# Two-layer hybrid decoder trunk on Trainium2: gating activations, a sliding tile's row maximum and the order of filler work and gated tiles changed

## Chip, cores and metric
The kernel runs on one core of one Trainium2 chip. The metric is the device time of one execution in microseconds, here the median of three runs. The engines are TensorE (PE, with PEld for its weight loads), VectorE (DVE), ScalarE (ACT), GpSimd (POOL) and SyncE (SP), whose queue issues nearly all DMA.

## What is computed
Two layers over 1024 positions of width 1024. Each layer projects once, runs three causal token mixers on parts of the projection, gates each and sums the three; then comes an output projection, a norm and a second gated addition (cut here).

```python
u = rms_norm(x, norm_pre[l]) @ w_in[l]
(a_q, a_k, a_v, a_z, b_q, b_kv, b_kr, b_z, c_q, c_k, c_v, c_z, g) = split(u)
oa = diff_attention(...)              # 4 heads, two softmaxes each
ob = mla_attention(...)               # 8 heads, low-rank keys and values
oc = sliding_window_attention(...)    # 8 heads, 128 keys back, a sink in the softmax
gates = sigmoid(g).reshape(B, S, 3, D)
y = (gates[:, :, 0] * ((oa * silu(a_z)) @ w_br_a[l])
     + gates[:, :, 1] * ((ob * silu(b_z)) @ w_br_b[l])
     + gates[:, :, 2] * ((oc * silu(c_z)) @ w_br_c[l]))
x = x + rms_norm(y @ w_out[l], norm_post[l])
```

## The kernel before
Everything is kept transposed, channels on partitions, positions along the free axis in two halves (`hf`) of 512. A product in fp32 is made of three fast matmuls: each operand is split (`split`, L88) into a high part H (a cast on ACT) and a low part L = x - H (DVE, L93), and HH + HL + LH are summed in PSUM. PSUM has eight banks: two with the tag mm, three sc, two tr, one av.

A layer runs through these stages:
- **Dense stage.** Four `z_unit`s (L434) make z of mixer a: 128 channels each, 48 matmuls of 128x512, an evacuation (zs) by ACT, a store to DRAM. Then `seven` (L458) prepares sums and differences T of the hidden state and runs eight `pair`s (L484). A pair makes 256 channels with seven products instead of eight, 84 matmuls: in the bank X twice with weight block 1 (`wr` w1), in Y with S2, S3 and A22, in Z with S1 and S4, all made from w1 and a second raw block w2. u2, u3 and p1 (tiles `po`) collect X, Y and Z. Here the pairs make gates 0 and 1.
- **sw** (L627): 16 sliding tiles. Each makes scores of four heads in two sc banks (L689), adds the bias (L691), takes the maximum (L692, with the sink at L697), exponentiates on ACT (L703), transposes and multiplies by the values.
- **da** (L813), then **mla** (L922), which begins with `mla_entry` (L1008). Each mixer ends with `put_rows` (L605): reciprocals of its row sums are transposed on PE and stored.
- **merge** (L1096): for each of the three mixers 16 `gated` tiles (8 j and hf; four channel blocks by two halves), then eight column blocks of 128, two halves each, 12 matmuls per half: 192 matmuls a mixer. `gated` loads o, z and the reciprocals rb, forms o * rb * silu(z) and splits it.
- **tail**: output projection and the second gate.

Beside the mixers run **fillers**: generators of dense units (here z of b and c, gate 2: 16 units of 48 matmuls). `fill` (L335) advances them by six matmuls at places in the mixers; FILL gives how many steps at which place and RATE which share of them goes to these units. What is left is drained at the start of the merge.

A scheduler puts each engine's instructions into a fixed order from the order in the program; what stands under `high_priority` comes earlier. At run time every engine, and SP's queue, takes its instructions in that order, so one that waits holds up all behind it.

Of the kernel before, what the change touches and what calls it, by code (L numbers as in the profile page):

```python
# [60 lines left out]
class Builder:  # L61
# [372 lines left out]
    def z_unit(self, l, b, j):  # L434
        W = self.load_w(self.win(l, OFF[b + "z"] + j * P))

        def evac(hf, ps):
            st = self.zp.tile([P, 512], F32, tag="zs", bufs=2, name=self.uid("zs"))
            self.copy("a", st, ps)
            self.nc.sync.dma_start(  # L440
                self.z_d[l, b][j * P:(j + 1) * P, hf * 512:(hf + 1) * 512], st)

        yield from self.unit(W, KT, self.hT, evac)

    def g_unit(self, l, bi, j):
        W = self.load_w(self.win(l, OFF["g"] + bi * D + j * P))
# [11 lines left out]
    def seven(self, l):  # L458
        nc = self.nc
        with ExitStack() as ctx:  # L460
            pl = self.pool("seven", ctx)
            T = [[tuple(pl.tile([P, 512], F32R, name=self.uid("T")) for _ in range(2))
                  for _ in range(4)] for _ in range(4)]
            for k in range(4):
                r = {}
                for hf in range(2):
                    for c in range(2):
                        H, L = self.hT[hf][4 * c + k]
                        r[c, hf] = pl.tile([P, 512], F32, tag="po", bufs=5, name=self.uid("po"))
# [10 lines left out]
            for bi in range(2):  # L480
                for j in range(0, KT, 2):
                    self.drain(self.pair(l, pl, T, OFF["g"] + bi * D + j * P, self.g_d, bi * D + j * P))

    def pair(self, l, pl, T, c, dst, r0):  # L484
# [5 lines left out]
        w1, w2 = self.load_raw(self.win(l, c)), self.load_raw(self.win(l, c + P), pl, tag="s")  # L490
# [36 lines left out]
        def put(a, hf, src):  # L527
            nc.sync.dma_start(dst[r0 + a * P:r0 + (a + 1) * P, hf * 512:(hf + 1) * 512], src)
# [24 lines left out]
        with self.tc.high_priority():  # L553
# [73 lines left out]
    def sw(self, l):  # L627
        nc = self.nc
        with ExitStack() as ctx:
# [13 lines left out]
            R = pl.tile([P, 8, 8], F32, name=self.uid("R"))  # L643
# [30 lines left out]
            self.put_rows(pl, l, "c", R.rearrange("p h i -> p (h i)"))  # L674
            self.fill(FILL[5], True)

    def sw_tile(self, l, pl, g, i, bias, sink, qs, kA, kB, Vp):
# [6 lines left out]
        for c in range(2):  # L684
# [6 lines left out]
            nc.vector.tensor_tensor(ps[:, :, k0:], ps[:, :, k0:], bias[:, h0:h0 + 2, k0:], ALU.add)  # L691
            nc.vector.tensor_reduce(mx[:, 2 * c:2 * c + 2], ps[:, :, k0:], AX.X, ALU.max)  # L692
# [4 lines left out]
        nc.vector.tensor_tensor(mx, mx, sk, ALU.max)  # L697
# [618 lines left out]
```

## Time and profile before

| | before |
|---|---|
| median of 3 runs | 2736.88 us (2733.1 to 2738.93) |
| profiled execution | 2740.26 us |
| its span | 2738.5 us |
| mean granted TensorE clock | 0.984 |
| PE busy | 2619.7 us, 96% |
| DVE busy | 1703.1 us, 62% |
| ACT busy | 1265.1 us, 46% |
| POOL busy | 393.2 us, 14% |

A busy time is the union of an engine's instructions. PE's share of 96% is a mean over stages: in some it is busy for whole stretches, in others it waits, and the granted clock tells where the chip let it run below full speed. The rows name a tile by the program's name with its buffer number left out, so `sc<-sc,swb` is the sliding tile's bias add.

### The profile page before, as it was taken

The page shows a single profiled execution, that of the slowest core. Times are in us where ns is not written, and L with a number is a line of the kernel's source. Part 1 is how long each engine was busy: PE and PEld are TensorE (multiplying, and loading weights), DVE is VectorE, ACT ScalarE, POOL GpSimd, SP SyncE. Part 2 cuts the span into 40 slices and gives each one's busy share as a digit, 9 for nine tenths or more (in the row PEclk, how much of TensorE's full clock was granted, in tenths as well). Part 3 has the DMA queues.
Part 4 walks back from the last instruction along what each step waited for, and adds up shares of the span by engine and source line. Part 5 has one row for each costly group of instructions (what it writes and reads, how often), then busy time and mean ns, then how long its engine had stood idle before and what let it go on. Part 6 is the DMA issues. An engine that isn't in the chain of part 4 may idle for free.

```text
span 2738.5 us, 35853 instructions
## 1 busy us (share of the span) xinstructions
PE 2619.7 (96%) x12832; PEld 2132.5 (78%) x12832; DVE 1703.1 (62%) x3232; ACT 1265.1 (46%) x2759; POOL 393.2 (14%) x359
## 2 busy tenths in 40 slices
PE   8999979999999988999999999899999999889999
PEld 6888758887877866788878887688887877668887
DVE  8653665776587655655566537567756876456653
ACT  5322543555477643334443226445545765333332
POOL 2000000000010034315410000000000111351441
PEclk9999979999999999999999999999999999999999
DMA  6333222211011376443333331222110114764442
GB/s 207 99 112 85 64 51 63 66 49 59 24 31 27 91 236 212 145 141 119 125 120 100 112 85 53 80 57 58 53 54 21 28 42 154 238 191 130 139 121 93
DMA packets 296818, 269.21 MB, mean 98 GB/s; under 512 B 24272, under 2 KB 237456, under 8 KB 296512
## 3 DMA queue, kind: packets, MB, share of 16 engines
q1 hardware_dynamic: 295568, 262.19, 31.8%
q0 software_dynamic: 1072, 4.73, 0.6%
q8 instruction: 101, 1.65, 0.3%
q14 instruction: 77, 0.63, 0.1%
HBM read 194.93 MB, written 61.44 MB: 94 GB/s over the span
## 4 chain that ended last, share of the span: by engine, by line
PE 76%; DVE 9%; DMA 5%; ACT 4%; issue 3%; POOL 2%; SPq 0%; DVEq 0%; POOLq 0%; ACTq 0%
PE mm L305 44%; PE sc L104 8%; PE mm L519 8%; PE av L774 5%; PE tr L790 3%; PE sc L519 3%; DVE wL L93 2%; PE sc L305 2%; ACT wH L78 1%; DVE o L1159 1%; PE tr L711 1%; POOL o L1158 1%; DVE po L473 1%; DMA wr<-w_in 1%; DMA sig<-g_d 1%
## 5 line engine op out<-in xcount | busy, mean ns | idle before, releaser
L305 PE MATMUL mm<-big,wH 128*128 128x512 f32 x3456 | 1111.9, 397 | 23.3 <-ACT zs L78 14.2
L305 PEld LDWEIGHTS mm<-big,wH 128*128 128x128 f32 x3456 | 642.4, 189 | 152.8 <-ACT zs L78 19.7
L305 PE MATMUL mm<-big,wL 128*128 128x512 f32 x1728 | 683.4, 396 | 3.3 <-DVE wL L93 3.2
L93 DVE TENSOR_TENSOR wL<-wr,wH 128x1024 fp32r<-128x1024 f32 (+3 forms) x252 | 268.7, 1073 | 246.2 <-ACT wH L78 238.5
L305 PEld LDWEIGHTS mm<-big,wL 128*128 128x128 f32 x1728 | 326.6, 189 | 66.6 <-DVE wL L93 4.5
L78 ACT CAST wH<-wr 128x1024 fp32r<-128x1024 f32 (+3 forms) x252 | 211.9, 851 | 289.2 <-PE mm L305 231.7
L761 ACT ACTIVATE e<-sc,st 128x512 f32<-128x512 f32 (+3 forms) x384 | 221.7, 582 | 96.1 <-DVE st L758 62.7
L755 DVE TENSOR_REDUCE st<-sc 128x1 f32<-128x512 f32 (+3 forms) x384 | 208.6, 551 | 5.8 <-PE sc L104 1.7
L78 ACT CAST wtH<-tr 128x512 fp32r<-128x512 f32 x204 | 115.5, 589 | 94.1 <-PE tr L790 72.4
L790 PE MATMUL tr<-cm,e 128*128 128x128 f32 x864 | 148.9, 275 | 1.1 <-ACT e L761 1.0
L93 DVE TENSOR_TENSOR wtL<-tr,wtH 128x512 fp32r<-128x512 f32 x204 | 137.7, 681 | 15.0 <-ACT wtH L78 13.7
L305 PE MATMUL mm<-oH,wH 128*128 128x512 f32 x256 | 103.6, 405 | 20.6 <-DVE y L1128 14.8
L790 PEld LDWEIGHTS tr<-cm,e 128*128 128x128 f32 x864 | 107.2, 142 | 19.6 <-ACT e L761 6.9
L519 PE MATMUL mm<-T,aH 128*128 128x512 f32 x384 | 119.0, 390 | 1.2 <-ACT T L78 1.1
L104 PE MATMUL sc<-kA,q 128*128 128x256 f32 (+3 forms) x320 | 106.2, 343 | 0.4
L305 PE MATMUL mm<-oL,wH 128*128 128x512 f32 x256 | 102.4, 400 | 0.0
L305 PE MATMUL mm<-oH,wL 128*128 128x512 f32 x256 | 102.0, 399 | 0.0
L104 PE MATMUL sc<-kB,q 128*128 128x256 f32 (+3 forms) x320 | 100.4, 323 | 0.0
L305 PE MATMUL mm<-og,wH 128*128 128x512 f32 x256 | 83.6, 409 | 13.6 <-DVE sig L1130 8.9
L1159 DVE TENSOR_TENSOR o<-o,sg 128x512 f32<-128x512 f32 x48 | 52.6, 1099 | 67.7 <-POOL o L1158 62.5
L1154 POOL TENSOR_TENSOR sg<-sg,z 128x512 f32<-128x512 f32 x48 | 70.2, 1466 | 169.3 <-ACT sg L1153 169.0
L78 ACT CAST aH<-S 128x512 fp32r<-128x512 f32 x64 | 39.5, 622 | 107.5 <-PE mm L519 63.7
(306 smaller groups left out, 4930.2 us busy)
## 6 DMA issues: line engine op xcount, KB each, us to landing
wr<-w_in SPq DMA_DIRECT2D x108, 512.0 KB, 3.9
sig<-g_d SPq DMA_DIRECT2D x48, 512.0 KB, 3.7
wr<-w_out SPq DMA_DIRECT2D x32, 512.0 KB, 4.1
wr<-w_ple_gate SPq DMA_DIRECT2D x32, 512.0 KB, 4.0
g_d<-zs SPq DMA_DIRECT2D x48, 256.0 KB, 2.2
g_d<-po SPq DMA_DIRECT2D x48, 256.0 KB, 2.2
kB<-kA SPq DMA_DIRECT2D x80, 128.0 KB, 2.7
x<-x SPq DMA_DIRECT2D x16, 512.0 KB, 6.1
```

What stands on the lines that cost most here:

```text
L78: nc.scalar.copy(out, in_)
L93: (nc.vector if le == "v" else nc.gpsimd).tensor_tensor(L, src, h, ALU.subtract)
L104: self.nc.tensor.matmul(ps, w, x, start=i == 0, stop=i == n - 1)
L305: self.nc.tensor.matmul(ps, w, x, start=i == 0, stop=i == n - 1)
L473: nc.vector.tensor_tensor(out, x, y, ALU.subtract)
L519: nc.tensor.matmul(ps, w, x, start=start and not i, stop=i == 11, skip_group_check=True)
L755: nc.vector.tensor_reduce(st[:, c:c + 1], ps[:, :w], AX.X, ALU.max, negate=len(ch) == 1)
L761: nc.scalar.activation(e[:, k0:k0 + w], pss[c][:, :w], AF.Exp, bias=st[:, 0:1], accum_out=sums[:, c:c + 1])
L774: self.nc.tensor.matmul(av[:, 0:256], w, x, start=self.first and not i, stop=last and i == len(terms) - 1)
L790: self.nc.tensor.transpose(tr[:, (2 * a + q) * P:(2 * a + q + 1) * P], ws[q][:, kt * P:(kt + 1) * P], self.ident)
L1154: nc.gpsimd.tensor_tensor(sg, sg, z, ALU.mult)
L1159: nc.vector.tensor_tensor(o, o, sg, ALU.mult)
```

## The change
- **Activations.** `z_unit` (now of mixer a alone) stores silu(z): sigmoid on ACT, product on DVE. The pairs now make z of b and c, with a sigmoid on ACT and a product on GpSimd, and gate 0, with its sigmoid. The fillers are gates 1 and 2, their weights' low halves on GpSimd (`le="g"`). The merge takes the sigmoid only for those two.
- **The pair.** The product Z x S1 is written ahead of Y x S3; the second raw weight block has one buffer instead of two, the split parts three instead of four.
- **Sliding tiles.** Bias sum and maximum are one instruction per head, which starts from the sink; the step with the sink alone is gone. RATE for this part is 1.0 instead of 0.5.
- **Row sums.** The transposes of c and a are put off (`rows_due`) to behind the next stage's first group, with filler in between.
- **Merge.** `gated` has two parts: the loads, with GpSimd's o * rb, and the rest. The first part runs two tiles ahead, tiles of the next mixer are made during the present one, weight blocks are loaded two column blocks ahead, and the products rotate over seven banks.

The diff, cut to what the text below speaks of:

```diff
-FILL = (3, 2, 2, 1, 1, 5, 3)
-
-RATE = dict(c=0.5, a=0.35, b=0.3)
+FILL = (3, 2, 2, 1, 1, 5, 4)
+
+RATE = dict(c=1.0, a=0.35, b=0.35)
...
         def evac(hf, ps):
+            nc = self.nc
             st = self.zp.tile([P, 512], F32, tag="zs", bufs=2, name=self.uid("zs"))
-            self.copy("a", st, ps)
-            self.nc.sync.dma_start(
-                self.z_d[l, b][j * P:(j + 1) * P, hf * 512:(hf + 1) * 512], st)
+            nc.scalar.activation(st, ps, AF.Sigmoid)
+            nc.vector.tensor_tensor(st, ps, st, ALU.mult)
+            nc.sync.dma_start(self.z_d[l, b][j * P:(j + 1) * P, hf * 512:(hf + 1) * 512], st)
...
-        W = self.load_w(self.win(l, OFF["g"] + bi * D + j * P))
+        W = self.load_w(self.win(l, OFF["g"] + bi * D + j * P), le="g")
...
+            z = [self.z_unit(l, "a", j) for j in range(4)]
+            self.by_halves(*z[0:2])
+            self.drain(*z[2:4])
...
+            for b in "bc":
+                for j in (0, 2):
+                    self.drain(self.pair(l, pl, T, OFF[b + "z"] + j * P, self.z_d[l, b], j * P, True))
+            for j in range(0, KT, 2):
+                self.drain(self.pair(l, pl, T, OFF["g"] + j * P, self.g_d, j * P, False))
...
-        w1, w2 = self.load_raw(self.win(l, c)), self.load_raw(self.win(l, c + P), pl, tag="s")
+        w1, w2 = self.load_raw(self.win(l, c)), self.load_raw(self.win(l, c + P), pl, bufs=1, tag="s")
...
-            H, L = (pl.tile([P, 4, P], F32R, tag=t, bufs=4, name=self.uid(t)) for t in ("aH", "aL"))
+            H, L = (pl.tile([P, 4, P], F32R, tag=t, bufs=3, name=self.uid(t)) for t in ("aH", "aL"))
...
         def put(a, hf, src):
-            nc.sync.dma_start(dst[r0 + a * P:r0 + (a + 1) * P, hf * 512:(hf + 1) * 512], src)
+            to = dst[r0 + a * P:r0 + (a + 1) * P, hf * 512:(hf + 1) * 512]
+            sg = pl.tile([P, 512], F32, tag="sg", bufs=2, name=self.uid("sg"))
+            nc.scalar.activation(sg, src, AF.Sigmoid)
+            if silu:
+                nc.gpsimd.tensor_tensor(sg, src, sg, ALU.mult)
+            nc.sync.dma_start(to, sg)
...
         with self.tc.high_priority():
-            c11 = self.zp.tile([P, 512], F32, tag="zs", bufs=2, name=self.uid("zs"))
+            c11 = new()
             self.copy("a", c11, X)
             put(0, 0, c11)
             S1 = parts(s1)
+        Z = self.psum("sc")
+        yield from product(Z, S1, T[0], start=True)
+        with self.tc.high_priority():
+            A22 = parts(a22)
         yield from product(Y, S3, T[2])
         u3 = new()
         with self.tc.high_priority():
             V.tensor_tensor(u3, Y, p1, ALU.add)
-            A22 = parts(a22)
-        Z = self.psum("sc")
-        yield from product(Z, S1, T[0], start=True)
-        with self.tc.high_priority():
             V.tensor_tensor(u3, Z, u3, ALU.add)
...
-            self.put_rows(pl, l, "c", R.rearrange("p h i -> p (h i)"))
+            self.rows_due = lambda: self.put_rows(pl, l, "c", R.rearrange("p h i -> p (h i)"))
             self.fill(FILL[5], True)
...
-            nc.vector.tensor_reduce(mx[:, 2 * c:2 * c + 2], ps[:, :, k0:], AX.X, ALU.max)
+            for hh in range(2):
+                h = h0 + hh
+                nc.vector.tensor_tensor_reduce(
+                    ps[:, hh, k0:], ps[:, hh, k0:], bias[:, h, k0:], 1.0, sink[:, h:h + 1],
+                    ALU.add, ALU.max, mx[:, 2 * c + hh:2 * c + hh + 1])
...
-        nc.vector.tensor_tensor(mx, mx, sk, ALU.max)
...
                 self.weave(g, 1)
+                if self.rows_due:
+                    self.rows_due()
+                    self.rows_due = None
...
+            self.rows_due = lambda: self.put_rows(pl, l, "a", ms)
...
-                                      lambda kt: (WH[:, kt], WL[:, kt])), 1)
+                                      lambda kt: (WH[:, kt], WL[:, kt])), 1, not hf and t < 2)
+                if self.rows_due:
+                    self.rows_due()
+                    self.rows_due = None
...
+            def begin():
+                if order:
+                    begun.append(self.gated(l, pl, *order.pop(0), og, tiles))
+                    next(begun[-1])
+
+            def finish(n):
+                for _ in range(n):
+                    if begun:
+                        for _ in begun.pop(0):
+                            pass
+                    begin()
+
...
+                W = tuple(self.w.tile([P, 4, 256], F32R, tag=t, bufs=2, name=self.uid(t)) for t in ("wH", "wL"))
+                with self.tc.high_priority():
+                    self.split(*W, raw)
+                return W
+
...
+            finish(2)
+            n = len(self.fillers)
+            for k in range(n):
+
+                finish(8 * (k + 1) // n - 8 * k // n)
+                if k == n - 1:
+                    next(self.fillers[0])
+                    raw = load()
                 self.drain(self.fillers[0])
+            W = split(raw)
             for bi, b in enumerate("abc"):
...
-                    if j % 2 == 0:
-                        W = self.load_w(io["w_br_" + b][l][:, j * P:(j + 2) * P])
                     r0 = bi * D + j * P
                     s = pl.tile([P, S], F32, tag="sig", bufs=4, name=self.uid("sig"))
                     nc.sync.dma_start(s, self.g_d[r0:r0 + P, :])
-                    nc.scalar.activation(s, s, AF.Sigmoid)
+                    if bi:
+                        nc.scalar.activation(s, s, AF.Sigmoid)
+                    if j % 2 == 0:
+                        raw = load()
+                    else:
+                        nxt = split(raw)
 
...
-                    self.drain(self.unit(W, 4, og, evac, c0=(j % 2) * P))
-
-    def gated(self, l, pl, b, hf, j, out):
+                    for hf in range(2):
+
+                        tag = ("mm", "sc", "tr", "mm", "sc", "tr", "sc")[(16 * bi + 2 * j + hf) % 7]
+                        self.drain(self.unit(W, 4, og[b], evac, c0=(j % 2) * P, halves=(hf,), tag=tag))
+                    if j % 2:
+                        W = nxt
+
+                    finish((2, 1, 1, 1, 1, 1, 1, 0)[j])
...
-        o = pl.tile([P, 512], F32, tag="o", bufs=2, name=self.uid("o"))
-        z = pl.tile([P, 512], F32, tag="z", bufs=2, name=self.uid("z"))
+        o, z, rb = (pl.tile([P, 512], F32, tag=t, bufs=3, name=self.uid(t)) for t in ("o", "z", "rb"))
...
-        sg = pl.tile([P, 512], F32, tag="sg", bufs=2, name=self.uid("sg"))
-        nc.scalar.activation(sg, z, AF.Sigmoid)
-        nc.gpsimd.tensor_tensor(sg, sg, z, ALU.mult)
+        nc.sync.dma_start(z, self.z_d[l, b][src])
+        if b != "a":
...
+            nc.gpsimd.tensor_tensor(o, o, rb, ALU.mult)
+        yield
+        if b not in og:
+            tiles(b)
         if b == "a":
-            nc.vector.scalar_tensor_tensor(o, o, self.vecs[l]["sub"], rb, ALU.mult, ALU.mult)
+            self.keep(nc.vector.scalar_tensor_tensor(o, o, self.vecs[l]["sub"], rb, ALU.mult, ALU.mult))
+            nc.vector.tensor_tensor(o, o, z, ALU.mult)
         else:
-            nc.gpsimd.tensor_tensor(o, o, rb, ALU.mult)
-        nc.vector.tensor_tensor(o, o, sg, ALU.mult)
-        self.split(*out, o)
+            self.keep(nc.vector.tensor_tensor(o, o, z, ALU.mult))
+        self.split(*og[b][hf][j], o)
...
-            self.units = self.later(*[z[b, j] for b in "bc" for j in range(4)],
-                                    *[self.g_unit(l, 2, j) for j in range(KT)])
+            self.units = self.later(*[self.g_unit(l, bi, j) for bi in (1, 2) for j in range(KT)])
```

**How the order moves.** First DVE in the dense stage, from u2 of a pair on. Before (`aL` is the low half of a split part, `S` a sum or difference of weight blocks, `wr` a raw block, `po_951` u3):

```order
L538 TENSOR_TENSOR po_912<-mm_885,po_898 128x512
L93 TENSOR_TENSOR aL_975<-S_972,aH_974 128x512
L504 TENSOR_TENSOR S_1052<-wr_1006,wr_1008 128x512
L93 TENSOR_TENSOR wL_1149<-wr_1144,wH_1148 128x1024
L549 TENSOR_TENSOR po_951<-mm_885,po_898 128x512
L93 TENSOR_TENSOR aL_1019<-S_1016,aH_1018 128x512
L554 TENSOR_TENSOR po_951<-sc_957,po_951 128x512
```

After (`wr_902` is this pair's second block, `wr_1052` the next pair's, `po_1003` u3):

```order
L568 TENSOR_TENSOR po_944<-mm_917,po_930 128x512
L93 TENSOR_TENSOR aL_988<-wr_902,aH_987 128x512
L93 TENSOR_TENSOR wL_1205<-wr_1200,wH_1204 128x1024
L529 TENSOR_TENSOR S_1058<-wr_1052 128x512
L529 TENSOR_TENSOR S_1060<-S_1058,wr_1050 128x512
L93 TENSOR_TENSOR aL_1013<-S_1010,aH_1012 128x512
L529 TENSOR_TENSOR S_1096<-wr_1050,wr_1052 128x512
L583 TENSOR_TENSOR po_1003<-mm_917,po_930 128x512
```

The sum over the next pair's second block now stands four rows ahead of u3, and two rows behind the last reader of this pair's.

Next PE near the end of layer 0's sliding part. Before, scores (`sc`), transposes (`tr`) and the product with the values (`av`) follow each other:

```order
L104 MATMUL sc_3207<-kB_1850,q_1856 128x256
L711 MATMUL tr_3231<-cm,e_3147 128x128
L711 MATMUL tr_3240<-cm,e_3147 128x128
L104 MATMUL av_3249<-wtH_3236,Vp_1857 128x512
L104 MATMUL av_3249<-wtL_3237,Vp_1857 128x512
L104 MATMUL av_3249<-wtH_3245,Vp_1857 128x512
L104 MATMUL av_3249<-wtL_3246,Vp_1857 128x512
```

After, with the filler units' `mm`:

```order
L305 MATMUL mm_3541<-big_151,wH_3537 128x512
L104 MATMUL av_3423<-wtH_3410,Vp_1957 128x512
L305 MATMUL mm_3541<-big_150,wL_3538 128x512
L305 MATMUL mm_3503<-big_160,wH_3443 128x512
L305 MATMUL mm_3503<-big_161,wH_3443 128x512
L305 MATMUL mm_3503<-big_160,wL_3444 128x512
L305 MATMUL mm_3503<-big_162,wH_3443 128x512
L104 MATMUL av_3423<-wtL_3411,Vp_1957 128x512
L104 MATMUL av_3423<-wtH_3419,Vp_1957 128x512
L305 MATMUL mm_3503<-big_163,wH_3443 128x512
```

Matmuls of filler units stand between those of a tile; layer 0's sliding part holds 192 of them, before 120. On GpSimd, from the start of that part, now:

```order
L662 DMA sink_1938<-sw_sinks 128x8
L664 DMA swb_1940<-bias_d 128x8x256
L93 TENSOR_TENSOR wL_2668<-wr_2665,wH_2667 128x1024
L93 TENSOR_TENSOR wL_3033<-wr_3030,wH_3032 128x1024
L195 TENSOR_SCALAR sub_2802<-subln_2775 128x1
L93 TENSOR_TENSOR wL_3251<-wr_3248,wH_3250 128x1024
L195 TENSOR_SCALAR sub_2814<-subln_2784 128x1
L185 TENSOR_TENSOR pr_2794<-lm_2792 128x128
L185 TENSOR_TENSOR pr_2806<-lm_2804 128x128
L93 TENSOR_TENSOR wL_3444<-wr_3441,wH_3443 128x1024
```

Before, the rows of `wL` were not there; each of the low halves stands in one queue with the small operations of the set-up (`sub`, `pr`).

Last, DVE in layer 0's merge. Before, where the evacuations of mixer a (`y`) meet the gated tiles of mixer b (`o`, `og`):

```order
L1159 TENSOR_TENSOR o_10063<-o_10063,sg_10070 128x512
L1128 TENSOR_TENSOR y_9168<-mm_9728,sig_9725 128x512
L93 TENSOR_TENSOR og_10000<-o_10063,og_9999 128x512
L1159 TENSOR_TENSOR o_10077<-o_10077,sg_10084 128x512
L93 TENSOR_TENSOR og_10002<-o_10077,og_10001 128x512
L1128 TENSOR_TENSOR y_9176<-mm_9742,sig_9725 128x512
L1128 TENSOR_TENSOR y_9169<-mm_9759,sig_9756 128x512
L1159 TENSOR_TENSOR o_10091<-o_10091,sg_10098 128x512
```

After:

```order
L1204 TENSOR_TENSOR y_9398<-mm_9824,sig_9820 128x512
L1204 TENSOR_TENSOR y_9406<-sc_9838,sig_9820 128x512
L1243 TENSOR_TENSOR o_9744<-o_9744,z_9745 128x512
L93 TENSOR_TENSOR og_9728<-o_9744,og_9727 128x512
L1243 TENSOR_TENSOR o_9855<-o_9855,z_9856 128x512
L1204 TENSOR_TENSOR y_9399<-tr_9880,sig_9874 128x512
L93 TENSOR_TENSOR og_9730<-o_9855,og_9729 128x512
L1204 TENSOR_TENSOR y_9407<-mm_9894,sig_9874 128x512
```

The product with the activated z is the gated tile's first step on DVE now, and the banks of the products change from row to row (`mm`, `sc`, `tr`).

## Rows read from the trace of the kernel before

**Rows 1.** The page, parts 1 and 2: engines; granted clock in 40 slices.
```profile
PE 2619.7 (96%) x12832; PEld 2132.5 (78%) x12832; DVE 1703.1 (62%) x3232; ACT 1265.1 (46%) x2759; POOL 393.2 (14%) x359
...
PEclk9999979999999999999999999999999999999999
```

**Rows 2.** The view of cores: span and mean granted clock.
```profile
core 0: 2738.5 us, clock 0.984
```

**Rows 3.** The chain in order of time: start, length (us), engine, operation, line.
```profile
366.14 1.05 PE sc L104 x4
...
379.13 1.05 PE sc L104 x4
...
1161.87 57.49 PE mm L305 x252
```

**Rows 4.** Stretches: length, busy us (x instructions), PEclk, DMA share, GB/s.
```profile
core 0: us, PE busy (x) PEld busy (x) DVE busy (x) ACT busy (x) POOL busy (x), PEclk, DMA share, GB/s
120.00:200.00 80.00, 80.00 (x355) 66.26 (x354) 44.00 (x64) 21.57 (x33) 0.00 (x0) 1.00 0.37 114
320.00:420.00 100.00, 82.04 (x332) 60.22 (x331) 56.62 (x149) 44.03 (x126) 2.00 (x8) 0.83 0.25 61
660.00:700.00 40.00, 35.35 (x177) 30.79 (x176) 15.97 (x44) 13.62 (x35) 0.94 (x1) 0.91 0.20 62
960.00:1120.00 160.00, 136.60 (x563) 107.03 (x562) 83.47 (x91) 58.95 (x83) 69.99 (x48) 0.97 0.66 215
980.00:1000.00 20.00, 15.80 (x68) 12.43 (x68) 5.83 (x7) 8.06 (x11) 3.11 (x3) 1.00 0.88 294
1740.00:1760.00 20.00, 13.57 (x44) 8.31 (x43) 10.85 (x21) 8.36 (x20) 0.64 (x4) 0.74 0.50 127
2020.00:2080.00 60.00, 56.66 (x282) 50.08 (x281) 27.51 (x80) 20.09 (x58) 1.29 (x4) 0.97 0.14 42
2300.00:2460.00 160.00, 138.87 (x564) 110.03 (x563) 86.20 (x92) 60.48 (x86) 69.43 (x47) 0.95 0.69 220
```

**Rows 5.** DVE by form, 220 to 420: busy us, mean ns | idle before.
```profile
L691 DVE TENSOR_TENSOR sc<-sc,swb 128x512 f32<-128x512 f32 x28 | 19.3, 692 | 18.4 <-PE sc L104 13.2 <-ACT e L703 4.0 <-PE tr L711 1.1
...
L692 DVE TENSOR_REDUCE mx<-sc 128x2 f32<-128x512 f32 x28 | 19.0, 682 | 0.1
...
L697 DVE TENSOR_TENSOR mx<-mx,sink 128x4 f32<-128x4 f32 x16 | 2.4, 150 | 0.1
...
L691 DVE TENSOR_TENSOR sc<-sc,swb 128x256 f32<-128x256 f32 x4 | 1.6, 422 | 0.0
```

**Rows 6.** Waits of TensorE, 320 to 420: us in total, times, longest.
```profile
PE mm L305 <- DVE kA L93: 3.5, 1, 3.5
PE mm L305 <- DVE wL L93: 2.7, 1, 2.7
```

**Rows 7.** Waits of TensorE, 960 to 1120, the merge of layer 0.
```profile
PE mm L305 <- DVE y L1128: 8.8, 6, 3.3
PE mm L305 <- ACT zs L78: 8.3, 6, 2.7
```

**Rows 8.** The page, part 5, gated product: busy, mean ns | idle before.
```profile
L1159 DVE TENSOR_TENSOR o<-o,sg 128x512 f32<-128x512 f32 x48 | 52.6, 1099 | 67.7 <-POOL o L1158 62.5
```

**Rows 9.** By form over the whole run: GpSimd and DVE.
```profile
L1154 POOL TENSOR_TENSOR sg<-sg,z 128x512 f32<-128x512 f32 x48 | 70.2, 1466 | 169.3 <-ACT sg L1153 169.0
...
L93 DVE TENSOR_TENSOR wL<-wr,wH 128x1024 fp32r<-128x1024 f32 x188 | 241.0, 1282 | 239.2 <-ACT wH L78 231.8 <-PE tr L1229 3.3 <-PE mm L305 3.0
```

**Rows 10.** The page, part 6: loads, count, KB each, us from issue to landing.
```profile
wr<-w_in SPq DMA_DIRECT2D x108, 512.0 KB, 3.9
sig<-g_d SPq DMA_DIRECT2D x48, 512.0 KB, 3.7
```

**Rows 11.** DVE by line and form, 120 to 280, the dense stage.
```profile
L93 DVE TENSOR_TENSOR aL<-S,aH 128x512 fp32r<-128x512 f32 x19 | 13.0, 682 | 0.0
...
L504 DVE TENSOR_TENSOR S<-wr 128x512 f32<-128x512 f32 x4 | 2.8, 693 | 0.1
```

More of the change, by code (lines that the diff above doesn't have):

```diff
@@ L480, in seven, with slot, split @@
[L480 to L484, printed above, removed]
+            T = [[None] * 4 for _ in range(4)]
+            def slot(dt=F32):
+                return pl.tile([P, 512], dt, tag="T", bufs=35, name=self.uid("T"))
+            def split(t, k, src):
+                T[t][k] = slot(F32R), slot(F32R)
+                self.split(*T[t][k], src)
@@ new lines, in seven, with whole, new @@
+            V = nc.vector
+            def whole(out, c, hf, k):
+                H, L = self.hT[hf][4 * c + k]
+                V.tensor_tensor(out, H.bitcast(F32), L.bitcast(F32), ALU.add)
+            def new():
+                return pl.tile([P, 512], F32, tag="po", bufs=5, name=self.uid("po"))
+            kept = []
+            for k in range(4):
+                b11, t1 = new(), new()
+                b12, t2, b22 = slot(), slot(), slot()
+                whole(b11, 0, 0, k)
+                whole(b12, 0, 1, k)
+                whole(b22, 1, 1, k)
+                V.tensor_tensor(t1, b12, b11, ALU.subtract)
+                split(0, k, t1)
+                V.tensor_tensor(t2, b22, t1, ALU.subtract)
+                split(1, k, t2)
+                kept.append((b12, t2, b22))
@@ new lines, in seven @@
+            for k, (b12, t2, b22) in enumerate(kept):
+                t4, t3 = new(), new()
+                whole(t4, 1, 0, k)
+                V.tensor_tensor(t4, t4, t2, ALU.subtract)
+                V.tensor_tensor(t3, b22, b12, ALU.subtract)
+                split(2, k, t3)
+                split(3, k, t4)
+            for b in "bc":
[3 more added lines that the diff above has]
+                self.drain(self.pair(l, pl, T, OFF["g"] + j * P, self.g_d, j * P, False))
@@ L489, in pair @@
+    def pair(self, l, pl, T, c, dst, r0, silu):
         nc, V = self.nc, self.nc.vector
-        w1, w2 = self.load_raw(self.win(l, c)), self.load_raw(self.win(l, c + P), pl, tag="s")
+        w1, w2 = self.load_raw(self.win(l, c)), self.load_raw(self.win(l, c + P), pl, bufs=1, tag="s")
         H1 = self.w.tile([P, KT, P], F32R, tag="wH", bufs=2, name=self.uid("wH"))
@@ L1101, in merge, with tiles @@
             y = [[pl.tile([P, 512], F32, name=self.uid("y")) for _ in range(KT)] for _ in range(2)]
-            while self.fillers:
+            og, begun = {}, []
+            order = [(b, hf, j) for b in "abc" for hf in range(2) for j in range(4)]
+            blocks = [(b, j) for b in "abc" for j in range(0, KT, 2)]
+            def tiles(b):
+                if b == "b":
+                    og[b] = [[tuple(self.big.tile([P, 512], F32R, tag="big", bufs=32, name=self.uid("og"))
+                                    for _ in range(2)) for _ in range(4)] for _ in range(2)]
+                else:
+                    og[b] = [[tuple(pl.tile([P, 512], F32R, tag=t, bufs=8, name=self.uid(t))
+                                    for t in ("oH", "oL")) for _ in range(4)] for _ in range(2)]
@@ new lines, in begin, with load @@
+            def begin():
[8 more added lines that the diff above has]
+                    begin()
+            def load():
+                if blocks:
+                    b, j = blocks.pop(0)
+                    return self.load_raw(io["w_br_" + b][l][:, j * P:(j + 2) * P])
@@ new lines, in split @@
+            def split(raw):
+                if raw is None:
+                    return
+                W = tuple(self.w.tile([P, 4, 256], F32R, tag=t, bufs=2, name=self.uid(t)) for t in ("wH", "wL"))
[9 more added lines that the diff above has]
+                    raw = load()
@@ L1103, in merge @@
                 self.drain(self.fillers[0])
+            W = split(raw)
             for bi, b in enumerate("abc"):
-                if b == "b":
-                    og = [[tuple(self.big.tile([P, 512], F32R, tag="big", bufs=32, name=self.uid("og"))
-                                 for _ in range(2)) for _ in range(4)] for _ in range(2)]
-                else:
-                    og = [[tuple(pl.tile([P, 512], F32R, tag=t, bufs=8, name=self.uid(t))
-                                 for t in ("oH", "oL")) for _ in range(4)] for _ in range(2)]
@@ L1112, in merge @@
-                for hf in range(2):
-                    for j in range(4):
-                        self.gated(l, pl, b, hf, j, og[hf][j])
                 if b == "c":
```

31 lines of the change are left out of this document (5 added, 26 removed).

## Prediction
> **What bounds the kernel now.** I read the page's busy times and granted clock first. TensorE is busy for 2619.7 of 2738.5 us [rows 1] at a mean clock of 0.984 [rows 2]; no other engine passes 62%. The change leaves TensorE's work as it is: both orders hold 12,720 matmuls, a dense filler matmul takes 57.49/252 = 0.228 us [rows 3] wherever it stands, so moving one gains nothing by itself. What can be gained is time in which TensorE waits, or works at the lower of its two clock levels (1.2 instead of 2.4 GHz). I call it the loss of a stretch: its length minus busy time times granted clock. For the whole run it is 2738.5 - 2619.7 x 0.984 = 160.7 us.
>
> Then I asked for it stretch by stretch [rows 4]. Sliding part of layer 0 (320 to 420): 100 - 82.04 x 0.83 = 31.9. End of the same part in layer 1 (1740 to 1760): 10.0. From da to mla (660 to 700, 2020 to 2080): 7.8 + 5.0 = 12.8. Merges (960 to 1120, 2300 to 2460): 27.5 + 28.1 = 55.6. These are the stretches that the edits touch, and they hold 110.3 of the 160.7. The dense stage, which the edits touch too, has no loss: 80.00 of 80 us busy at full clock.
>
> **Part 1, sliding part of layer 0: 31.9 to 12, so -19.9.** The chain of waits comes back to the same step two tiles later, after 379.13 - 366.14 = 12.99 us [rows 3]; their own matmuls are about 5.5 us of that (32 short ones at half of 0.228, 8 whole ones), so some 7.5 us per two tiles are free for other work. The order now puts 192 filler matmuls into this part instead of 120: 72 x 0.228 = 16.4 us more work of the kind that leaves the merge. That fits into 31.9 us, and it keeps the clock up, which stood at 0.83 here. The chain itself gets shorter. Per tile DVE did 2 x (0.692 + 0.682) + 0.150 = 2.90 us; now four passes of 128x256 and four readouts of 128x1. No fused pass is in the trace. Nearest are the 128x256 add at 0.422 and, for a readout, the small operation at 0.150 [rows 5]: 4 x 0.572 = 2.29, so -0.61 per tile, some -4 on the seven tiles that nothing covered. If readouts cost nothing it is 1.69, and if a pass costs twice the add it is 4 x 0.844 = 3.38, which turns -4 into +3. I take 2.29, since both are DVE reads of the same shapes. Two waits stay, kA (3.5) and wL (2.7) [rows 6], and some of the lower clock with them: 12 is those 6.2 us and as much again.
>
> **Part 2, sliding part of layer 1: 10.0 to 5, so -5.** By the order layer 1 had fillers nearly throughout; what is left is its last 20 us, where a wait like the 3.5 on kA remains.
>
> **Part 3, da to mla: 12.8 to 6, so -6.8.** The transposes of the row sums waited for a chain of short operations. Now 17 filler matmuls (3.9 us) stand in front of it, and 30 more per layer between the groups of the mla entry. They cover the chain's short waits, not the lower clock around them.
>
> **Part 4, merges: 55.6 to 24, so -31.6.** TensorE waits there for y (8.8 us in 160), for the zs copies (8.3) and others [rows 7]. All are late releases of one of two banks, because DVE stands in order behind a gated tile: over the run it waited 62.5 us for GpSimd's product o [rows 8], which follows sg x z, 1466 ns each [rows 9], which follows a sigmoid of z, which follows loads with two buffers. In the new order z arrives activated, GpSimd's product is issued two tiles ahead, a third of the gates needs no sigmoid, and the banks number seven, so that an evacuation may be late by 7 x 2.74 = 19 us. These waits go. What is late next is DMA. One mixer has 192 x 0.228 = 43.8 us of matmuls and loads 8 gates of 512 KB [rows 10], 8 tiles o and z of 256 KB each, as many rb, and four weight blocks of 512 KB: 12.58 MB, so 287 GB/s. That holds for mixers a and b (while b's tiles are loaded, then c's); c needs half. The merge moved 215 and 220 GB/s while waiting for other things, and 294 in its best 20 us, at a DMA share of 0.88 [rows 4]. I take the middle of 215 and 294, 254: 49.5 us, 5.7 late, twice, so 12 per merge. Bounds: 0 if 287 is held, and 28 per merge, today's loss, at 217. The Trainium skill, "DMA: Bandwidth & Descriptors", section Specifications, gives about 358 GB/s as HBM's limit for a core; by that figure the estimate would be 0 late and the sum 24 us lower, which lies in rival B below. No stretch of this trace comes near it, and 294/0.88 = 334.
>
> **Part 5, dense stage: +7.** Mostly hidden, as TensorE has no wait there, but three things come nearer. (a) Eight evacuations per layer of z a now need 0.69 us of DVE beside ScalarE's, and the splits for the seven products start behind them: +1 per layer. (b) GpSimd's silu, 4 x 1466 ns in a pair of 84 x 0.228 = 19.2 us, has a whole product of slack, and so have the sigmoids: 0. (c) The second raw weight block of a pair has one buffer instead of two. DVE's row aL_988 is its last reader; only then can the next pair's block be loaded, 3.9 us [rows 10], and the sum S_1058 that needs it stands four rows ahead of u3 (po_1003), which TensorE waits for before the next product into the same bank. Counted from the start of the product Y x S2: it ends at 2.74, u2 and aL_988 take DVE to about 4.5, the block lands at 8.5, four operations at 0.69 [rows 11] lead to 11.3, u3 ends at 12.0. Without that, u3 would follow the end of Y x S3 (10.94, its results some 0.2 later) and end at 11.8, when the four matmuls of the next pair that the order puts there (0.9 us) are through at 11.86. So about 0.25 us late in 14 pairs: 3.5, and with the start of each stage 5. Each further us of that load costs 14: bounds 0 and 18.
>
> **Part 6, other moves: 0.** The 32 filler units of g1 and g2 have their low halves on GpSimd, which takes 188 - 32 = 156 on DVE; GpSimd was busy 14%. Moved fillers bring their loads to a stretch with a DMA share of 0.25.
>
> Sum: -19.9 - 5 - 6.8 - 31.6 + 2 + 5 = -56.3. The profiled execution took 2740.3, so 2684.0; the median of the three runs lies 3.4 below it: **2681 us**.
>
> **Rivals.** *A, DMA takes the merge's waits over.* Everything else happens, but each merge keeps about 28 us, because loads at 217 GB/s end last. For it: mean rates of 215 and 220, and one queue that issues every load in order, so that one load that waits for a buffer holds up the next. Against: the 294. Price 31.6: 2681 + 31.6 = **2712**. *B, cover is deeper than I allow.* Losses end at 6 and 3 (sliding), 3 (transitions), 4 per merge: 25.9 + 7 + 9.8 + 47.6 = 90.3 gained, 2 lost: **2649**. For it: a stretch with full filler, as 120 to 200, loses nothing. *C, GpSimd is late with the low halves, and the kernel is slower.* A 128x512 product there takes 1466 ns against DVE's 692, so a 128x1024 low half some 2.93 us against 1.28 [rows 9], and GpSimd works in order: wL_3444 stands behind pr, which waits for a late load, others behind the zeroing of da's diagonal tiles. TensorE, in order too, meets such a unit in the middle of a tile. Exposed in full, 32 x 2.93 = 93.8 and 2681 + 94 = **2775**; it decides from 56.3/32 = 1.76 us per unit. Against: units are begun a tile or more ahead (wL_2668 and wL_3033 in the order), and GpSimd is idle there. The Trainium skill, "GPSIMD Engine Reference", section 4.1, says to keep two-input elementwise work on VectorE, about 2x faster; the trace agrees (1466 against 692), and by that rule this edit alone loses. It does so only where a split ends last. *D, the single weight buffer costs more.* At a landing 2 us later, +28 instead of +5: **2704**; on DVE two-input operations beside GpSimd's took 1099 ns instead of 692 (o<-o,sg against S) [rows 8, 11], so the four operations could add 1.6 us more.
>
> **How the numbers follow.** A measurement of this kernel can tell about 0.2%, 5.5 us, from no change. Chances: the forecast (2662 to 2697) 0.48; A and D, 2697 to 2728, 0.24; B, 2640 to 2662, 0.12; C and worse sums, over 2742, 0.08; within 5.5 us of 2737, 0.05; under 2640, 0.03. For 8 in 10 the range takes the forecast, most of A and D (to 2722) and of B (from 2648). Faster 0.87, same 0.05, slower 0.08. The term with the widest bounds is part 4 (0 to 56 left of 55.6), then part 5c.
>
> **What would show it.** Same stretches, same arithmetic: sliding 12, transitions 6, merge 12 each with waits on loads instead of y and zs. Fused pass near 0.42 us. In the pair, a wait of TensorE for po of 0.2 to 0.3 us, and full clock. Part 4 is wrong if DMA's share in the merge stays near 0.66 while TensorE waits; part 5 if the dense stage shows over 18 us of waits in all; part 6 if TensorE waits for GpSimd's wL in sum over 10 us.

## The result and the profile after

The changed kernel takes 2654.1 us (median of four runs, 2652.84 to 2655.15) against 2737.9 (2733.1 to 2740.58): ratio 0.9696, interval 0.9679 to 0.9712, so 83.8 us less. That is inside the range (2648 to 2722), but outside the forecast's own 2662 to 2697 and closest to rival B (2649).

The page and the view of cores of the changed kernel, as in [rows 1, 2]:

```profile
PE 2587.8 (98%) x12832; PEld 2120.4 (80%) x12832; DVE 1659.6 (63%) x3312; ACT 1265.6 (48%) x2761; POOL 452.6 (17%) x375
...
PEclk9999999999999999999999999999999999999999
...
core 0: 2652.2 us, clock 0.995
```

By the prediction's arithmetic the loss of the whole run is 2652.2 - 2587.8 x 0.995 = 77.3 us, before it was 160.7. TensorE's work is what it was (2574.9 us at full clock, before 2577.8), so the gain is loss that went, as forecast. The stretches that answer to [rows 4]; columns as there:

```profile
320.00:420.00 100.00, 93.99 (x460) 76.40 (x459) 55.25 (x180) 51.40 (x136) 9.25 (x11) 0.97 0.33 83
660.00:700.00 40.00, 36.77 (x183) 32.21 (x182) 14.35 (x29) 12.86 (x27) 5.67 (x3) 0.96 0.27 82
984.00:1064.00 80.00, 80.00 (x349) 65.19 (x348) 53.14 (x61) 23.49 (x29) 35.07 (x23) 1.00 0.95 293
1064.00:1124.00 60.00, 60.00 (x260) 48.62 (x259) 44.66 (x62) 27.10 (x34) 11.37 (x8) 1.00 0.44 137
1380.00:1400.00 20.00, 12.38 (x47) 9.39 (x47) 19.91 (x34) 8.85 (x15) 0.00 (x0) 0.84 0.13 40
1720.00:1740.00 20.00, 19.72 (x88) 16.05 (x88) 7.18 (x14) 5.72 (x12) 2.45 (x2) 1.00 0.34 93
1980.00:2040.00 60.00, 54.47 (x263) 47.91 (x262) 24.06 (x63) 19.14 (x51) 5.66 (x3) 0.94 0.19 57
2296.00:2440.00 144.00, 144.00 (x626) 117.11 (x625) 101.93 (x125) 51.69 (x65) 48.38 (x31) 1.00 0.74 233
```

| stretch (loss, us) | before | forecast | after |
|---|---|---|---|
| sliding part, layer 0 (320 to 420) | 31.9 | 12 | 100 - 93.99 x 0.97 = 8.8 |
| sliding part, layer 1 (last 20 us) | 10.0 | 5 | 0.3 |
| da to mla (660 to 700; 1980 to 2040) | 12.8 | 6 | 4.7 + 8.8 = 13.5 |
| merges (984 to 1124; 2296 to 2440) | 55.6 | 24 | 0 |
| dense stage, both layers | 3.2 | 10.2 | 16.9 |

The last row is summed over slices of 20 us (20 to 260 and 1340 to 1560 before; 20 to 260 and 1280 to 1520 after). Ahead of the first merge, 960 to 984 lost 1.2 us more while fillers were drained. TensorE's longest waits in the changed kernel, over the run:

```profile
PE tr L425 <- DMA cm<-cm: 12.0, 1, 12.0
PE mm L544 <- ACT po L78: 8.4, 2, 7.5
PE mm L305 <- ACT zs L78: 4.4, 6, 1.2
PE tr L263 <- ACT sincos L252: 4.2, 1, 4.2
PE mm L544 <- DVE po L583: 3.9, 8, 1.3
PE mm L305 <- ACT WH L78: 2.7, 2, 2.0
PE tr L639 <- DVE ms L898: 2.2, 1, 2.2
PE mm L305 <- POOL wL L93: 1.9, 2, 0.9
```

The waits for y, sig, kA and most of those for zs [rows 6, 7] are gone. The first is the wait for the first load, which both kernels have. New are the second, in the first pairs of the dense stage; po L583, which is u3; and the one for sincos L252, in the 20 us that hold most of what is left in layer 0's sliding part, 20 - 15.85 x 0.83 = 6.8 of the 8.8 us. There DVE, in order, had stood behind a product of GpSimd (L185) whose load came late.

```profile
340.00:360.00 20.00, 15.85 (x71) 13.27 (x69) 14.17 (x52) 5.30 (x9) 2.92 (x2) 0.83 0.23 66
```

### The profile page after: what moved, and what is told of

It is laid out like the page before. It is cut to its first block, busy times and chain, and to the rows that moved or that the text cites. A ratio compares the mean times of both kernels' runs of the same rounds, so it can differ in the third digit from the quotient of the medians.

```text
span 2652.2 us, 35930 instructions
## 1 busy us (share of the span) xinstructions
PE 2587.8 (98%) x12832; PEld 2120.4 (80%) x12832; DVE 1659.6 (63%) x3312; ACT 1265.6 (48%) x2761; POOL 452.6 (17%) x375
## 5 line engine op out<-in xcount | busy, mean ns | idle before, releaser
L305 PE MATMUL mm<-big,wH 128*128 128x512 f32 x3456 | 1106.5, 395 | 4.9 <-ACT zs L78 2.4
L93 DVE TENSOR_TENSOR wL<-wr,wH 128x1024 fp32r<-128x1024 f32 (+2 forms) x220 | 222.6, 1021 | 234.4 <-ACT wH L78 229.8
L93 POOL TENSOR_TENSOR wL<-wr,wH 128x1024 fp32r<-128x1024 f32 x32 | 77.4, 2423 | 501.7 <-ACT wH L78 336.6
L544 PEld LDWEIGHTS mm<-T,aH 128*128 128x128 f32 x384 | 70.6, 188 | 26.3 <-DVE po L583 9.8
L544 PE MATMUL mm<-big,wH 128*128 128x512 f32 x256 | 82.9, 397 | 8.4 <-ACT po L78 8.4
L93 POOL TENSOR_TENSOR kL<-vT,kH 64x512 fp32r<-64x512 f32 x32 | 42.2, 1318 | 265.6 <-ACT kH L78 200.2
L379 POOL TENSOR_TENSOR acc<-acc,sq 128x512 f32<-128x512 f32 x36 | 56.8, 1577 | 176.2 <-ACT sq L378 176.2
L913 DVE TENSOR_TENSOR sc<-sc,dab 128x256 f32<-128x256 f32 (+1 forms) x128 | 52.4, 412 | 47.8 <-PE sc L104 46.6
L305 PE MATMUL mm<-WH,big 128*128 128x416 f32 x256 | 76.9, 370 | 3.6 <-ACT WH L78 2.7
```

The source lines that it names most:

```text
L93: (nc.vector if le == "v" else nc.gpsimd).tensor_tensor(L, src, h, ALU.subtract)
L305: self.nc.tensor.matmul(ps, w, x, start=i == 0, stop=i == n - 1)
L379: (nc.gpsimd if eng == "g" else nc.vector).tensor_tensor(st, st, sq, ALU.add)
L544: nc.tensor.matmul(ps, w, x, start=start and not i, stop=i == 11, skip_group_check=True)
L913: nc.vector.tensor_tensor(ps[:, a - k0:w], ps[:, a - k0:w], bias[:, h, a - n + 256:k0 + w - n + 256], ALU.add)
```

## Experiments

All start from the changed kernel unless something else is named. Ratios are to the kernel before, measured beside it on the same chip; the changed kernel stands at 0.9696. One hundredth of the ratio is 27 us.

**two_banks.** The merge's rotation over seven banks taken back.

```diff
-                        tag = ("mm", "sc", "tr", "mm", "sc", "tr", "sc")[(16 * bi + 2 * j + hf) % 7]
+                        tag = "mm"
```

> The changed kernel with the merge's products in the two mm banks again instead of seven; gated tiles still in two parts, two tiles ahead. Theory (the merge's 58 us came from the look-ahead, which keeps DVE free to evacuate): one product is 12 x 0.228 = 2.74 us and an evacuation 0.69, so two banks are nearly enough; 2654 + 0 to 6 us. Rival (the seven banks carried it): 20 to 45 us come back, 2675 to 2700, as waits of TensorE for y and sig in the merge.

0.9730 (0.9712 to 0.9749): 9 us slower, between the two, nearer to the look-ahead. Its waits in layer 0's merge are short:

```profile
PE mm L305 <- ACT zs L78: 3.1, 2, 2.0
PE mm L305 <- DVE sig L1206: 1.0, 1, 1.0
```

**one_part.** The look-ahead taken back, both the two tiles ahead and the next mixer's tiles during the present one: all eight gated tiles stand at their mixer's start.

```diff
-            finish(2)
...
-                finish(8 * (k + 1) // n - 8 * k // n)
...
+                for _ in range(8):
+                    begin()
+                    for _ in begun.pop(0):
+                        pass
...
-                    finish((2, 1, 1, 1, 1, 1, 1, 0)[j])
```

> The changed kernel with all eight gated tiles of a mixer written at that mixer's start, in one part, as before the change; activated z, seven banks and the rest stay. Theory (look-ahead carried the merge): each mixer starts with eight tiles that nothing covers, 35 to 55 us come back, 2690 to 2710. Rival (seven banks, or z that needs no sigmoid and no product on GpSimd, carried it): under 10 us, up to 2664.

0.9848 (0.9830 to 0.9866): 42 us come back, as the theory had it, though z arrives activated and the banks are seven. TensorE now waits for the high parts of the gated tiles (oH, og) where each mixer begins, and DMA stands at 0.61 in a stretch with 100 - 85.16 x 0.95 = 19 us of loss:

```profile
1020.00:1120.00 100.00, 85.16 (x345) 66.04 (x344) 59.38 (x75) 32.95 (x39) 42.47 (x29) 0.95 0.61 191
...
PE sc L305 <- ACT oH L78: 6.1, 1, 6.1
PE mm L305 <- ACT og L78: 4.1, 3, 1.9
```

So the merge's gain is the look-ahead first, the banks second. Which half of the look-ahead it is, no run separates.

**two_steps.** The fused pass taken back.

```diff
-            for hh in range(2):
-                h = h0 + hh
-                nc.vector.tensor_tensor_reduce(
...
+            nc.vector.tensor_tensor(ps[:, :, k0:], ps[:, :, k0:], bias[:, h0:h0 + 2, k0:], ALU.add)
+            nc.vector.tensor_reduce(mx[:, 2 * c:2 * c + 2], ps[:, :, k0:], AX.X, ALU.max)
...
+        nc.vector.tensor_tensor(mx, mx, sk, ALU.max)
```

> The changed kernel with the sliding tile's bias sum and maximum as two instructions per bank again and the step with the sink. Theory (filler covers the tiles, their chain no longer ends last): 0 to 3 us. Rival (the shorter chain on DVE carried the sliding part's 23 to 35 us): 0.6 us in each of 32 tiles come back, 10 to 19 us, 2664 to 2673.

0.9745 (0.9728 to 0.9762): 13 us slower; my theory fell, and the rival has the size but not the way. The loss does not come back by 0.4 us in each tile: it stands in one place, the end of layer 0's sliding part, 20 - 13.08 x 0.73 = 10.5 us between 400 and 420. The stretch, and the waits of TensorE from 395 to 430:

```profile
400.00:420.00 20.00, 13.08 (x53) 8.51 (x52) 13.84 (x28) 11.03 (x30) 3.01 (x5) 0.73 0.33 86
...
PE mm L305 <- DVE kA L93: 3.4, 1, 3.4
PE tr L741 <- ACT e L733: 2.1, 1, 2.1
```

What differs there is the order: the fillers are used up earlier, and the last eight transposes of that part have none beside them (three products with the values, eight transposes, three products, the transpose of the row sums, one product, then 72 matmuls of da's first units). The changed kernel has filler between them to the end, and 14 matmuls of it behind the last product. And the wait for kA [rows 6] is back. The trace also shows something else, the sink's maximum (L727), min/median/max in ns:

```profile
L727 DVE TENSOR_TENSOR mx<-mx,sink x16: 143/150/2135, 276.9 to 408.0; 128x4 f32<-128x4 f32 x16
```

It took up to 2135 ns instead of 150, about as long as a low half on GpSimd (2407 ns mean in that stretch); another, at 408.01, ends with GpSimd's low half at 409.9. Two runs followed from this.

**two_steps_dve.** two_steps, with `le="g"` taken out of `g_unit` too.

> two_steps with the low halves of the filler units' weights on DVE as in low_on_dve. In two_steps the small maximum with the sink, 128x4, took up to 2135 ns instead of 150, as long as a low half on GpSimd takes. Theory (the two steps lose their 13 us because that operation and GpSimd's product shut each other out, which the fused pass avoids): within 4 us of low_on_dve, 0.967 to 0.970. Rival (the order leaves the last tiles of layer 0 without filler and the wait for kA behind them, whatever GpSimd does): still 8 to 15 us slower than low_on_dve, 0.971 to 0.9745. In its order the last two tiles have no filler matmul between them.

0.9729 (0.9715 to 0.9742), low_on_dve (below) 0.9682: 13 us again. Without GpSimd's low halves the maximum takes 164 ns at most, so the collision is real, but the time stays. The loss stands at the uncovered end again (20 - 13.37 x 0.67 = 11.0 us between 400 and 420, kA 3.5).

**two_steps_cover.** two_steps, with more filler behind the last tile.

```diff
...
-FILL = (3, 2, 2, 1, 1, 5, 4)
+FILL = (3, 2, 2, 1, 1, 11, 4)
...
```

> As two_steps (sum and maximum apart again), with eleven instead of five filler steps behind the last sliding tile, so that filler matmuls stand in the order between the matmuls of the last tile of layer 0, as they do in the changed kernel and did not in two_steps. Theory (what two_steps lost, some 13 us, was the uncovered last tile and the wait for kA behind it, not the length of the instructions): 0.970 to 0.972 of before, within 4 us of the changed kernel. Rival (the fused pass itself shortens what ends last): 0.9735 to 0.9755, as two_steps.

0.9866 (0.9845 to 0.9888): 46 us slower than the changed kernel, which neither expected. The last tile is covered now, and TensorE waits for no e there, but no filler stands behind the last product, kA (3.6) stays, and there are losses in many other places (680 to 780: 100 - 89.00 x 0.95 = 15; both merges: 5 and 7). 161 filler matmuls are left for layer 0's merge instead of 190. It doesn't tell the two theories apart: that the order and not the length of the instructions costs the 13 us is read from the orders and no run shows it alone. Where all of its 46 us come from is open.

**old_rate.** FILL and RATE of before.

> The changed kernel with the filler rates and steps of before; fewer filler matmuls in the sliding parts, more drained at the merge's start. Theory (filler covers the sliding tiles): the loss of layer 0's sliding part goes from 11 back to 25 to 30 us, 2668 to 2675. Rival (fused pass or the low halves on GpSimd did it): under 5 us, up to 2659.

0.9750 (0.9729 to 0.9772): 15 us slower, as the theory had it, though the loss from 320 to 420 rises to 100 - 87.93 x 0.90 = 20.9 and not to 25 to 30. What is new is at 380 to 420 (7.6 + 5.4 us), with the wait for kA of 3.5 again. Taking back the rate or the fused pass costs nearly the same, in the same place.

**low_on_dve.** Low halves of the filler units' weights on DVE.

```diff
-        W = self.load_w(self.win(l, OFF["g"] + bi * D + j * P), le="g")
+        W = self.load_w(self.win(l, OFF["g"] + bi * D + j * P))
```

> The changed kernel with the low halves of the 32 filler units' weights on DVE again. Theory (GpSimd hides 2.4 us each, DVE has room): within 4 us of the changed kernel, 0.968 to 0.971. Rival C of the prediction (GpSimd is late with them): faster by 5 us or more. A third: DVE's queue in the sliding part is too full for them, slower by 5 to 12 us.

0.9682 (0.9665 to 0.9699): no difference that the intervals allow. GpSimd is not late with them, and DVE does not miss the room.

**p1_own** and **p1_own_and_more**, for the new wait of layer 1's first pair.

```diff
-                return pl.tile([P, 512], dt, tag="T", bufs=35, name=self.uid("T"))
+                return pl.tile([P, 512], dt, tag="T", bufs=33, name=self.uid("T"))
...
-        p1 = new()
+        p1 = pl.tile([P, 512], F32, tag="p1", bufs=2, name=self.uid("p1"))
```

The second also has `le="g"` for T2 and T3, and the operations between da's square sums and `put_rows` inside `rows_due`.

> The changed kernel with a tag of its own, two buffers, for the copy p1 of a pair's first product, paid for with two slots of T. Theory (the 7.5 us wait of layer 1's first pair is p1's buffer, which the preparation of T holds, so that ScalarE's copy stands behind casts that wait for DVE): that wait goes, -5 to -8 us, 0.9665 to 0.968. Rival (DVE's preparation of T as such ends last): the wait moves to the next product, 0 to -2 us.

> p1_own, with the low halves of T2 and T3 on GpSimd (1.3 to 1.5 us each instead of 0.69 on DVE) and with the chain of short operations behind da's square sums moved behind the first group of the mla entry. Theory: 5 to 8 us for the first pair of layer 1, 2 to 5 for the preparation and 3 to 6 for the transition, which lost 11 us in layer 1: 2640 to 2648, 0.964 to 0.967. Rival (the waits are taken over by the next one in line): within 4 us of p1_own.

0.9707 (0.9689 to 0.9725) and 0.9694 (0.9677 to 0.9711): no gain. The wait stayed in the first pair, for copies and u2 (L568). TensorE's waits from 1370 to 1425, first of p1_own, then of p1_own_and_more:

```profile
PE mm L544 <- ACT po L78: 6.9, 1, 6.9
PE mm L544 <- DVE po L568: 1.0, 1, 1.0
```

```profile
PE mm L544 <- DVE po L568: 5.6, 1, 5.6
PE mm L544 <- ACT po L78: 4.6, 1, 4.6
```

Why GpSimd's help brought nothing is in the DVE rows around the first pair. First p1_own_and_more, with GpSimd's low halves (1340 to 1420), then the changed kernel (1340 to 1400), both as line, form, count, busy us, mean ns:

```profile
L479 DVE TENSOR_TENSOR po<-big,big 128x512 f32<-128x512 f32 x8 | 7.6, 956 | 1.5 <-POOL big L93 1.5
L500 DVE TENSOR_TENSOR po<-T,T 128x512 f32<-128x512 f32 x4 | 3.8, 952 | 0.0
L499 DVE TENSOR_TENSOR po<-po,T 128x512 f32<-128x512 f32 x4 | 3.8, 948 | 0.0
...
L93 POOL TENSOR_TENSOR T<-po,T 128x512 fp32r<-128x512 f32 x8 | 13.8, 1751 | 38.5 <-DVE po L479 33.1 <-ACT T L78 5.4
```

```profile
L479 DVE TENSOR_TENSOR po<-big,big 128x512 f32<-128x512 f32 x8 | 5.5, 683 | 1.4 <-POOL big L93 1.4
L500 DVE TENSOR_TENSOR po<-T,T 128x512 f32<-128x512 f32 x4 | 2.7, 682 | 0.0
L499 DVE TENSOR_TENSOR po<-po,T 128x512 f32<-128x512 f32 x4 | 2.7, 682 | 0.0
```

Eight operations of 0.684 left DVE, 5.5 us; but 16 others with both inputs in SBUF took 0.95 instead of 0.683 while GpSimd's ran, 4.3 us, and those on weights more too. The Trainium skill, "GPSIMD Engine Reference", section 1 (Specifications), says that GpSimd shares its way into SBUF with VectorE, with contention for VectorE's instructions with two SBUF inputs; the rows agree, with 270 ns on each in the mean.

**early_g** and **early_g2.** low_on_dve, with one or two filler units drained between z a and the pairs, to give DVE 11 or 22 us to prepare T.

```diff
...
+            self.drain(self.g_unit(l, 1, 0))
             for b in "bc":
...
```

> low_on_dve with the first filler unit of each layer drained between z a and the pairs (48 matmuls, 11 us), so that DVE has that time to prepare T; 48 fewer are left for the merge (130 instead of 178). Theory (the first pair of each layer waits because DVE is busy throughout, not because of one buffer or one order): the 8 to 10 us lost around layer 1's first pair and the 2 to 3 of layer 0 go, 0.963 to 0.9655. Rival (the filler is missed in the merge, or the wait only moves): within 3 us of low_on_dve, 0.967 to 0.9695.

> early_g with two units ahead of the pairs; 82 filler matmuls, 19 us, are left for the merge, under which mixer a's eight gated tiles have to be made. Theory: the second unit finds no wait left to cover, and the merge begins to wait for gated tiles: same as early_g or up to 6 us slower. Rival (the preparation needs more than 11 us of cover): 2 to 5 us faster than early_g.

0.9675 (0.9662 to 0.9688) and 0.9753 (0.9740 to 0.9766). The theory on the first pair holds: in early_g TensorE is busy for all of 1380 to 1400 and waits there no more. But the merge loses what the pair gains, 130 matmuls being left instead of 178, and with 82 left it loses much more. Two slices of early_g, then one of early_g2, then what ScalarE waits for in early_g2 from 975 to 1024:

```profile
1380.00:1400.00 20.00, 20.00 (x89) 16.54 (x89) 19.31 (x31) 9.33 (x16) 0.00 (x0) 1.00 0.27 84
984.00:1004.00 20.00, 16.60 (x58) 12.48 (x57) 10.29 (x13) 3.43 (x5) 5.47 (x5) 0.83 0.89 263
```

```profile
984.00:1024.00 40.00, 31.48 (x113) 24.22 (x113) 25.51 (x34) 7.36 (x11) 9.90 (x7) 0.83 0.96 289
```

```profile
ACT wH L78 <- DMA wr<-w_br_a: 8.9, 2, 5.6
```

The weight block's high part comes late because its load does; DMA stands at 0.96. Here DMA does end last.

**dma_more.** Each gate block of the merge loaded twice.

```diff
+                    s2 = pl.tile([P, S], F32, tag="sig2", bufs=2, name=self.uid("sig2"))
+                    nc.sync.dma_start(s2, self.g_d[r0:r0 + P, :])
```

> The changed kernel with each gate block of the merge loaded a second time into a buffer that nothing reads. Mixers a and b then need 16.8 MB in 43.8 us, 383 GB/s, mixer c 239. The changed kernel moved 300 to 314 GB/s in the merge without a wait. Theory (that is close under what one core gets, some 320): 52 us instead of 44, 17 us more in each merge, 25 to 40 in all, 0.979 to 0.984. Rival (there is much room left): under 10 us, up to 0.973.

0.9770 (0.9754 to 0.9786): 20 us slower, between the two, nearer to the theory, whose 320 GB/s was too low. DMA is full, at 341 GB/s over 60 us (367 in the best 20), and TensorE loses 60 - 53.05 x 0.97 = 8.5 us in that stretch:

```profile
1020.00:1080.00 60.00, 53.05 (x223) 42.16 (x222) 39.41 (x42) 18.98 (x22) 30.87 (x21) 0.97 1.03 341
```

No kernel tried here is clearly faster than the changed one; the best, early_g, has an interval that overlaps its. No run takes back the activations, the pair's new order with its one buffer, or the transposes put off, each by itself: what the text says of these is read from rows.

## Why the prediction was right, and where it was not

- **Frame: right.** TensorE's work stayed, and the loss fell from 160.7 to 77.3 us.
- **Part 1 (31.9 to 12; measured 8.8): near in size, in part by luck, and too simple in kind.** Fillers and fused pass were costed as separate gains, the pass as 0.61 us per tile. It takes 487 ns and its readout 138 ns, so a tile 4 x 0.625 = 2.50 us, 0.40 less than before:

```profile
L723 DVE CUSTOM_DVE_ANT_0 sc<-sc,swb,sink 128x256 f32<-128x256 f32 x56 | 26.6, 487 | 10.1 <-PE sc L104 5.6 <-ACT e L735 2.0 <-PE tr L743 1.6
...
L723 DVE DVE_READ_ACCUMULATOR2_ANT mx<- 128x1 f32 x64 | 8.9, 138 | 0.0
```

  But either edit taken back costs 13 to 15 us, mostly at the end of the part, where the last tiles then stand without filler and kA follows late. They share one gain: both are needed, and their prices do not add up. The 12 was built on kA's wait and wL's (6.2 us) staying. Both went; kA's is absent where filler is left behind the last product and there where none is. What is left is 6.8 us around the wait for sincos, which the prediction does not name. low_on_dve has that wait too (4.0 us), so GpSimd's low halves don't make it; which edit does is open.
- **Part 2 (10 to 5; measured 0.3): too careful**, for the same wait.
- **Part 3 (12.8 to 6; measured 13.5): wrong.** Layer 0 went from 7.8 to 4.7, layer 1 from 5.0 to 8.8. The step that failed is "17 filler matmuls stand in front of it": I read that in layer 0 and took it for both. In layer 1's order the transpose of the sums follows the square sums directly, and TensorE waits 2.2 us for ms, at the lower clock around it. Moving the chain (p1_own_and_more) handed the wait to WH, 2.6 us.
- **Part 4 (55.6 to 24; measured 0): mechanism right, size wrong.** The waits for y and zs went, and one_part shows that the look-ahead did most of it (42 us). The term that failed is the DMA allowance of 254 GB/s. Without a wait the merge moved 293 GB/s over 80 us, at a share of 0.95, above the 287 of my own demand; the midpoint had no better reason than lying between two means of a merge that waited. It also left out that mixer a's tiles load under the filler that is left, 190 matmuls or 43 us. Rival A is nevertheless near: at 130 matmuls it begins (early_g), at 82 or with a third more load it happens. By the figure of the Trainium skill, "DMA: Bandwidth & Descriptors", section Specifications (about 358 GB/s as HBM's limit for a core), the loss would be 0, and it was. dma_more's 341 over 60 us lies below that figure, its best 20 us at 367 above.
- **Part 5 (+7; measured +13.7): (a) wrong, (b) wrong, (c) right in its sum by luck.** TensorE waited 3.9 us in all, eight times, for u3, against 3.5 forecast. But (c) put this down to the late block, in all 14 pairs. At most two of the eight waits (0.4 and 0.5 us) fit that: they follow a sum of usual length that waited over 1.2 us for its block. In the other six a DVE operation ahead of u3 took longer beside GpSimd's silu, which (b) had put at nothing: five times the first sum, 1.42 to 1.67 us instead of 0.69, once a low half, 2.32 instead of 1.23. From the timeline of the second pair (start, length in us), GpSimd, then DVE:

```profile
100.75 1.30 POOL L557 TENSOR_TENSOR sg<-po,sg 128x512 f32<-128x512 f32 x1 [6.67 <-ACT sg L555]
101.07 1.52 DVE L529 TENSOR_TENSOR S<-wr 128x512 f32<-128x512 f32 x1 [0.34 <-DMA wr<-w_in]
102.62 0.69 DVE L529 TENSOR_TENSOR S<-S,wr 128x512 f32<-128x512 f32 x1
```

  The six pairs that make gates and have a pair behind them, with the same one buffer and no silu, show one wait for u3. Rival D had named this cost. The start of the stage, (a), was put at +1 per layer; in layer 1 alone TensorE waited 7.5 us for a copy behind casts that waited for DVE, which was busy for 19.91 of 20 us there. I had counted the 0.69 us operations that were added and not what DVE had to do before the first product could go on.
- **Part 6 (0): right.** Two waits for wL on GpSimd, 1.9 us in all, and low_on_dve is no different. Rival C did not happen.
- **Numbers.** The errors of part 4 (24 too little gained), parts 1 and 2 (8), against parts 3 and 5 (14 too much), make 18 of the 27 us between 2681 and 2654; of the rest some 6, by slices of 20 us over both runs, lie in stretches for which I had no term. The range holds because it left room for rival B, and because errors of both signs met. Rival B had the right sum, with other parts: it took transitions at 3.

## What to carry to other kernels

When an engine's work stays the same, sum its lost time by stretch and ask of each stretch what ends last after the edit; do it in every layer, since a scheduled order differs from one to the next. Work that can stand anywhere is a stock: used in one place it is missing in another, and two edits that cover the same place do not add up. Before moving elementwise work to another engine, look in the trace for what its neighbour's instructions take beside it.

## What the runs showed of the hardware

- Beside GpSimd's products even a tiny DVE operation can be held up: one of 128x4 took up to 2135 ns instead of 150 (two_steps), and one of 128x128 with a single input 2298 instead of 227 (L224, at 343.9 in the changed kernel, beside a low half). Those of 128x512 with both inputs in SBUF took 950 instead of 683 in the mean (p1_own_and_more), enough to eat most of what the offloading had saved, and single ones in the pairs up to 1673.
- One core's DMA moved 293 GB/s over 80 us with blocks of 128 to 512 KB without holding up TensorE, and 341 over 60 us when more was asked.
- A fused sum and maximum of 128x256 took 487 ns, more than the 422 of the sum alone, and its result is read by an instruction of its own, 138 ns.
